# Attention's output product in seven block products per chunk, with weight sums made during attention

## The chip, the cores and the metric

The kernel runs on one core of one Trainium2 chip. The metric is the device time of one execution in microseconds (us). The engines are PE (matmul), PEld (its weight loads, which run beside PE), DVE (vector), ACT (scalar/activation), POOL (GpSimd) and SP, whose queue issues most DMAs. Times of the profile are counted from the start of the span, the stretch from the first to the last instruction of one profiled execution.

## The reference, cut to what matters

The computation is one step of a two-layer model over 256 context tokens and 1024 latent tokens, 1024 wide: first a gated linear attention layer (GLA), then a softmax attention layer with 8 heads of 128 and 2 key/value heads. The change concerns the last product of the attention layer:

```python
out_p = (attend_blocks(qp, kp, vp) * jax.nn.silu(gp)) @ att_w_out[i]
...
out_s = (attend_blocks(qs, keys, vals) * jax.nn.silu(gs)) @ att_w_out[i]
...
xp = xp + gt_p * out_p
xs = xs + gt_s * out_s
```

`att_w_out` is 1024 x 1024, all arrays are float32, and the rows are 256 + 1024 = 1280 tokens.

## The kernel before

**Number format.** A float32 operand is scaled by a power of two (`pow2`, from the largest magnitude) and split into two float16 parts: `hi` is an ACT copy with the scale, `lo` the rest, made by one DVE instruction from the float32 tile and `hi`. A product is then three matmuls for each 128 rows of the sum: hi·hi, hi·lo, lo·hi (`mm3`, line 247).

**The order of work.** All engines run their own queues in order. The order within a queue is chosen when the kernel is built, by a planner that simulates a timeline and takes instructions by program order plus an offset; the table `LATER` holds those offsets, by name of a step (`later("a.s0")`) and sometimes with an index. Memory of a closed pool is taken over by the next pool, and a tile there waits for the readers of the one that it replaces.

**The GLA loop** (about 100 to 475 us of the span). Beside its own work, `filler(slot)` fetches one 1 MB block of an attention weight (`stage`, into one of two `wst` tiles) in each slot of `AHEAD`, 14 in all, and `split_ahead` makes its scale (`scale`: four DVE reduces, `pow2`) and its split in four pieces of 512 elements, through the one `split` tile, and stores it in DRAM in float16 (`w_kv`, `w_q`, `w_g`, `w_o`). The last four blocks are the columns of `att_w_out` (`o0`, `o1`).

**Attention** (`attention`, about 700 to 1143 us). Ten steps n = 0 to 9, each one chunk of 256 tokens and one half of the heads; the second half takes the chunks in the order `OUT` = 1, 0, 2, 3, 4. A step has four heads e; a head has two `scores` (S in one of two three-bank tiles, maximum on DVE, exponential on ACT), two `rest` (the probabilities scaled and split on POOL or ACT and on DVE, then a DMA transposition from `phl` to `PT`) and, two heads later, `values`, which multiplies by the gate and stores the head's result in `og2_d`. `later` is a list of weight loads, one issued per head on SP. The split weights `o0` and `o1` are read back from step 6 and from step 9, into places that the gate and query weights have left. In step 9 the first chunk's row is loaded (`out2_load`) and prepared (`out2_prep`: two reduces, scale, split in two pieces of 1024) into the memory of `ropet`; after the ten steps two half tiles of chunk 1 (`out_piece`) are put among the last `values`.

**The last product** (`att_out`, about 1143 us to the end). Five chunks in the order `OUT`; a chunk has two token tiles, and a tile two halves of 512 output columns (`out_tile`, `residual`): 24 matmuls of 512 columns each into a bank `y`, then on DVE two multiplies (scale and gate) and one add of the residual row, and a store from ACT's queue. The next chunk's row is loaded and prepared beside the current chunk's matmuls.

Of the kernel before, what the change touches and what calls it, by code (L numbers as in the profile page):

```python
# [7 lines left out]
F16 = mybir.dt.float16  # L8
# [9 lines left out]
P = 128  # L18
# [26 lines left out]

OUT = (1, 0, 2, 3, 4)
# [18 lines left out]
    "a9.qr": 30,  # L65
    "a.s1": 30,
    "gate": -5,
    "a0.key": -85,
    "x.qr": -40,
    "z.val": 35,  # L70
    "o": -155,
    "x.q": -15,
    "a0.qr": 15,
# [3 lines left out]
    "a.q": -210,  # L77
    "x.mod": -60,
    "x.res": -225,
    "a.val": 20,  # L80
    "a9.gate": 5,
    "a9.q": -200,
    "a.s0": -25,
    "a.qr": -200,
    "a9.s1": -160,
    "a0.s1": 390,
    "pieces8": 95,
    "filler": -30,
    "a0.s0": 75,
    "at": -115,  # L90
    "a0.rest": 30,
    "a0.gate": 65,
    "silu": -150,
    "a9.s0": -20,
    "x.setup": -150,
    "a9.val": 5,
# [8 lines left out]
    "a0.q": 30,  # L105
    "wo3": 245,
    "x.key": -150,
# [14 lines left out]
    "a9.val.3": -80,  # L122
    "a.s0.1": -15,
    "a9.val.1": -5,
    "a9.rest.0": 25,
    "a9.rest.2": -60,
    "a.rest.0": 100,
    "a.val.1": 25,
    "z.val.0": -100,
    "a.q.0": -110,  # L130
    "a9.qr.1": 60,
    "z.val.1": 165,
    "a9.gate.2": 85,
    "a9.s1.0": -200,
    "a9.q.0": -210,
    "a9.gate.0": -5,
    "a9.q.2": 30,
    "a9.s1.2": -135,
    "a.s0.3": -100,
    "a.s1.0": 55,  # L140
    "a9.gate.3": 15,
    "a9.s1.3": -150,
    "z.prep": -5,
    "a9.s0.0": -25,
# [13 lines left out]
NAMES = ("kv", "q0", "g0", "q1", "g1", "o0", "o1")  # L158


class K:
# [36 lines left out]
    def pow2(self, mx, n=1, cross=True):  # L198
# [19 lines left out]
        nc.vector.tensor_scalar(s, e, -1, C268, ALU.mult, ALU.add)  # L218
        inv = self.t(sp, [P, n], I32, "p2i", bufs=12)
        nc.vector.tensor_scalar(inv, e, E14, None, ALU.subtract)  # L220
# [45 lines left out]
    def scale(self, st):  # L266
        nc = self.nc
        mx = self.t(self.small, [P, 4], F32, "wmx")
        for j in range(4):
            nc.vector.tensor_reduce(  # L270
                mx[:, j : j + 1], st[:, 2 * j : 2 * j + 2, :], AX.XY, ALU.max, apply_absolute_value=True
            )
        m = self.t(self.small, [P, 1], F32, "wm1")
        nc.vector.tensor_reduce(m, mx, AX.X, ALU.max)
        return self.pow2(m)
# [58 lines left out]


# [1024 lines left out]
    def rest(self, after=None):  # L1360
# [12 lines left out]
        if self.final:  # L1373
            parts = self.hT_lo[:, 0:2, :].rearrange("p k n -> p (k n)")
# [75 lines left out]
    def attention(self, wo, wk):  # L1450
# [4 lines left out]
        for n, (p, c) in enumerate(self.steps):  # L1455
# [4 lines left out]
            if n == 6:  # L1460
                wo.append(self.wload("o0", (0, 2), later))
            if n == 9:
                wo.append(self.wload("o1", 1, later))
            for e in range(4):
# [35 lines left out]
                if n == 9 and e == 1:  # L1500
                    xs, gs = ([self.hT_hi[:, a + j, 0:1024].bitcast(F32) for j in range(2)] for a in (0, 2))
                    with self.tc.issue_after(self.pt):
                        for j in range(2):
                            b = slice(512 * j, 512 * j + 512)
                            self.nc.sync.dma_start(gs[j], self.gt_d[1, 1:2, b].to_broadcast([P, 512]))
                            self.nc.sync.dma_start(xs[j], self.x1_d[2 * OUT[0], :, b])
                if n == 9 and e == 1:
                    first = self.ropet.rearrange("p a b d -> p (a b d)").bitcast(F16)
                    first = first.rearrange("p (j h t) -> p j h t", j=2, h=AH)
                    with self.later("z.prep"), self.tc.issue_after(self.last):  # L1510
                        self.prep = self.out2_prep(row, (first[:, 0], first[:, 1]))
        with self.tc.issue_after(self.pt):
            self.row, first = self.out2_load(OUT[1])
        with self.tc.issue_after(first):
            self.gt = self.gate_load(1)
        self.iw = self.inv_a[:, 10:14]
        wo[:] = [(hi, lo, 512) for hi, lo, _ in wo]
        for j, x in enumerate(xs):
            with self.later("z.out", f".{j}"):
                self.out_piece(OUT[0], 0, j, x, gs[j], wo)  # L1520
# [4 lines left out]
    def out2_load(self, c):  # L1525
        og = self.t(self.wst, [P, AH, 256], F32, "wst")
        return og, self.nc.sync.dma_start(og, self.og2_d[c]).ins

    def out2_prep(self, og, parts):
        nc = self.nc  # L1530
        hi, lo = parts
# [7 lines left out]
        s, inv = self.pow2(m)  # L1539
        for k in range(0, AH, 4):  # L1540
            nc.scalar.activation(hi[:, k : k + 4], og[:, k : k + 4], AF.Copy, scale=s)
            nc.vector.scalar_tensor_tensor(
                lo[:, k : k + 4], og[:, k : k + 4], s, hi[:, k : k + 4], ALU.mult, ALU.subtract
            )
        return hi, lo, inv

    def out_piece(self, c, j, cut, x, g, wo):
        nc = self.nc
        hi, lo, inv = self.prep
        i, a, b = 2 * c + j, slice(j * P, j * P + P), 512 * cut  # L1550
        o = self.O[0][0, i * P : i * P + P, :] if i < NTP else self.O[1][0, (i - NTP) * P : (i - NTP) * P + P, :]
        sc = self.t(self.small, [P, 4], F32, "rsc", bufs=2)
        nc.vector.tensor_scalar(sc, self.iw, inv, None, ALU.mult)
        ps = self.bank("mm")
# [400 lines left out]
```

## Time and profile before

| | |
|---|---|
| three runs | 1245.0, 1245.66, 1247.55 us; median 1245.66 |
| span of the profiled execution | 1240.9 us (the page gives no total of that execution beside it; the median run is 4.8 us longer than the span) |
| granted TensorE clock, mean | 0.997 |
| GLA loop | about 100 to 475 us |
| attention | about 700 to 1143 us |
| last product | 1143.7 us to the last DVE instruction at 1237.7 us |

A row of the table of stages gives the window, its length, then busy us and number of instructions of PE, PEld, DVE, ACT and POOL, the granted clock, the share of DMA time and GB/s. A group of instructions gives line, engine, operation, names written and read, shapes, count, then busy us, mean ns of one, idle us before and what ended it. In a tile's or a line's view the three numbers with slashes are the shortest, median and longest duration in ns. A DMA row ends in the median us from issue to landing. PE's busy time is modelled and covers short gaps.

### The profile page before, as it was taken

Reading aid. Unit: us, or ns where it says so; the run is one execution under the profiler, and the core shown is the slowest. Engines: PE = TensorE matmul, PEld = TensorE weight load, DVE = VectorE, ACT = ScalarE, POOL = GpSimd, SP = SyncE. Lnnn points to the kernel's source line nnn. Section 1 sums busy time; section 2 is a strip of 40 time slices with the busy share of each in tenths; the row PEclk is TensorE's granted clock in tenths of the full one; section 3 lists DMA queues with packets and bytes.
Section 4 is the critical chain, followed back from the end, with each engine's and each line's share of the span. In section 5 each row is a group of like instructions: output and inputs, shape, how many; then the busy total and the mean of one; then the engine's idle time right before and its main releaser. Section 6 shows DMA issues by size and latency. Waiting matters only on the chain. (4 is left out here: it accounts for less than half of the span.)

```text
span 1240.9 us, 22365 instructions
## 1 busy us (share of the span) xinstructions
PE 1190.7 (96%) x7990; PEld 778.3 (63%) x7990; DVE 944.9 (76%) x2177; ACT 687.0 (55%) x1694; POOL 320.5 (26%) x566
## 2 busy tenths in 40 slices
PE   5799999999999999799999999999999999989998
PEld 3467765655556566667776666776767666666444
DVE  4787779887888789976875787877767587786653
ACT  2565556665666657742333576666767676664110
POOL 0132122323321143311212443431322343311000
PEclk9999999999999999999999999999999999999999
DMA  9511566456555544489978787777958666979432
GB/s 378 196 69 73 196 202 228 127 185 203 175 191 164 189 132 161 112 186 307 204 174 203 178 163 138 132 145 133 199 124 161 124 118 132 205 139 246 158 137 85
DMA packets 318496, 210.14 MB, mean 169 GB/s; under 512 B 257158, under 2 KB 294702, under 8 KB 310064
## 3 DMA queue, kind: packets, MB, share of 16 engines
q1 hardware_dynamic: 311232, 191.18, 60.1%
q10 hardware_dynamic: 4688, 10.57, 2.2%
q0 software_dynamic: 2464, 6.95, 2.0%
q8 instruction: 63, 1.03, 0.3%
q14 instruction: 49, 0.40, 0.1%
HBM read 108.35 MB, written 38.96 MB: 119 GB/s over the span
## 5 line engine op out<-in xcount | busy, mean ns | idle before, releaser
L247 PEld LDWEIGHTS <-hT_hi 128*128 128x128 f16 x1920 | 187.6, 98 | 122.0 <-issue 5.6
L247 PE MATMUL mm<-whi,hT_hi 128*128 128x512 f16 (+1 forms) x576 | 200.2, 348 | 3.5 <-ACT gx L718 3.0
L247 PE MATMUL mm<-whi,hT_lo 128*128 128x512 f16 (+1 forms) x576 | 200.4, 348 | 0.0
L247 PE MATMUL mm<-wlo,hT_hi 128*128 128x512 f16 (+1 forms) x560 | 194.3, 347 | 0.7 <-DVE wlo L309 0.7
L247 PEld LDWEIGHTS <-whi 128*128 128x128 f16 x1232 | 120.3, 98 | 62.1 <-issue 2.2
L1344 PE MATMUL S<-kT,wst 128*128 128x512 f16 (+1 forms) x624 | 142.1, 341 | 4.1 <-ACT p L1352 4.0
L247 PE MATMUL mm<-hT_hi,whi 128*128 128x256 f16 (+1 forms) x480 | 141.1, 294 | 2.0 <-ACT gx L1392 2.0
L247 PE MATMUL mm<-hT_hi,wlo 128*128 128x256 f16 (+1 forms) x480 | 141.1, 294 | 0.0
L247 PE MATMUL mm<-hT_lo,whi 128*128 128x256 f16 (+1 forms) x480 | 141.1, 294 | 0.0
L1382 DVE SCALAR_TENSOR_TENSOR phl<-p,srec,phl 128x1280 f16<-128x1280 f32 (+1 forms) x79 | 105.3, 1332 | 40.6 <-ACT phl L1381 26.9
L247 PEld LDWEIGHTS <-hT_lo 128*128 128x128 f16 x960 | 94.1, 98 | 61.8 <-issue 1.1
L247 PE MATMUL mm<-PT,vh 128*128 128x256 f16 x672 | 114.6, 273 | 8.1 <-DMA PT<-phl 7.8
L1347 DVE TENSOR_REDUCE smx<-S 128x1 f32<-128x1280 f32 (+1 forms) x80 | 101.3, 1271 | 27.0 <-PE S L1344 26.9
L1352 ACT ACTIVATE p<-S,snb,acol 128x1280 f32<-128x1280 f32 (+1 forms) x80 | 99.1, 1239 | 12.5 <-DVE phl L1382 7.0
L1344 PEld LDWEIGHTS <-wst 128*128 128x128 f16 x624 | 61.4, 98 | 55.7 <-issue 6.9
L247 PE MATMUL mm<-PT,vl 128*128 128x256 f16 x336 | 91.6, 273 | 0.0
L1379 POOL TENSOR_SCALAR phl<-p,srec 128x1280 f16<-128x1280 f32 (+1 forms) x40 | 53.1, 1327 | 105.0 <-DVE srec L1370 57.1
L247 PEld LDWEIGHTS <-wlo 128*128 128x128 f16 x616 | 60.2, 98 | 29.2
L247 PEld LDWEIGHTS <-vh 128*128 128x128 f16 x672 | 65.1, 98 | 18.3 <-DMA PT<-phl 7.2
L1172 POOL TENSOR_TENSOR rope<-hx,ropet 128x64 f32<-128x64 f32 x160 | 51.2, 350 | 81.3 <-ACT hx L1308 63.8
L270 DVE TENSOR_REDUCE wmx<-wst 128x1 f32<-128x512 f32 x104 | 65.1, 677 | 3.5 <-DMA wst<-in_att_w 2.0
L238 POOL TENSOR_TENSOR hrs<-hrsa,mhalf 128x2 f32<-128x2 f32 x50 | 38.7, 775 | 106.8 <-DVE hrsa L236 106.5
(383 smaller groups left out, 2684.9 us busy)
## 6 DMA issues: line engine op xcount, KB each, us to landing
wada<-in_w_ada SPq DMA_DIRECT2D x16, 1024.0 KB, 5.4
wst<-in_att_w SPq DMA_DIRECT2D x14, 1024.0 KB, 5.3
wst<-in_gla_w_in SPq DMA_DIRECT2D x12, 1024.0 KB, 5.5
og_d<-og POOLq DMA_DIRECT2D x40, 128.0 KB, 2.8
wst<-og_d SPq DMA_DIRECT2D x5, 1024.0 KB, 6.0
og_d<-gx SPq DMA_DIRECT2D x37, 128.0 KB, 2.1
xr<-x_d SPq DMA_DIRECT2D x9, 512.0 KB, 3.3
out<-xr ACTq DMA_DIRECT2D x17, 256.0 KB, 2.0
```

Of the source, the lines that this page charges most:

```text
L238: nc.gpsimd.tensor_tensor(r, a, self.mhalf[:, 0:w], ALU.pow)
L247: self.pe = self.nc.tensor.matmul(out, a, b, start=k == 0 and j == 0, stop=k == n - 1 and j == 2).ins
L270: nc.vector.tensor_reduce(mx[:, j : j + 1], st[:, 2 * j : 2 * j + 2, :], AX.XY, ALU.max, apply_absolute_value=True)
L1172: nc.gpsimd.tensor_tensor(tv[:, h, :, w, :], xv[:, h, :, 1 - w, :], sn[:, :, w, :], ALU.mult)
L1344: nc.tensor.matmul(S[:, a : a + n], x, y, start=m == 0, stop=m == 2)
L1347: last = nc.vector.tensor_reduce(mx, S, AX.X, ALU.max).ins
L1352: nc.scalar.activation(p, S, AF.Exp, scale=self.sexp, bias=nb, accum_out=den)
L1379: nc.gpsimd.tensor_scalar(hi, p, r, 2.0 ** 14, ALU.mult, ALU.mult)
L1382: nc.vector.scalar_tensor_tensor(lo, p, r2, hi, ALU.mult, ALU.subtract)
```

## The change

The 256 tokens of a chunk, the 1024 rows of the sum and the 1024 columns are each taken in two halves, so that the chunk's product is one of 2 x 2 blocks. It is computed with seven block products and sums of blocks (the scheme of Strassen in Winograd's form), not eight block products.

*The weight.* `split_ahead` no longer handles `o0` and `o1`. Four blocks of `att_w_out`, each with 128 columns of either half, are fetched during attention, in steps 1, 3, 5 and 7 (`SPLIT`). At head 1 `split_out` makes the scale (with two bits of room for the sums) and splits three quarters as they are (B11, B21, B22); at head 3 `split_sums` makes four sums on POOL in place and splits them (T2, T3, T1, T4). Each part goes through one tile `opart` to `wo_d` in DRAM, 256 KB a store. Of the seven weights, 1 MB each, B11 and T2 are read back in step 8, T3, B21 and T1 in step 9, T4 and B22 in `att_out`.

*The rows.* `out2_prep` splits three of the chunk's four blocks as they are, makes four sums on POOL and splits those: seven ACT copies and seven DVE instructions of 512 elements. The first chunk is prepared in step 8.

*The products.* `product` has 12 matmuls of 512 columns; its moving operand is four pieces of 128 columns. `out_chunk` uses three banks: X, Y and Z. Products p6·T2 and p1·B11 are joined by an ACT copy and a DVE add, and later products add into a bank that DVE has changed. `finish` multiplies by the row's scale and the gate, adds the residual and stores, four times a chunk. The weight's scale goes into the gate row (`fold_gate`, POOL). Four products of the first chunk stand where the two half tiles did. The last head's split uses `ropet`.

Many offsets in `LATER` have other values and new names (`so`, `ss`, `e.t`, `e.prep`).

```diff
+SPLIT = (1, 3, 5, 7)
+PREPARE = 1
...
-NAMES = ("kv", "q0", "g0", "q1", "g1", "o0", "o1")
+NAMES = ("kv", "q0", "g0", "q1", "g1")
+B11, B21, B22, T2, T3, T1, T4 = range(7)
...
+    def split_part(self, g, s, m, b):
+        t = self.t(self.ew, [P, 2, 4, P], F16, "opart", bufs=1)
+        nc.scalar.activation(t[:, 0], b, AF.Copy, scale=s)
+        nc.vector.scalar_tensor_tensor(t[:, 1], b, s, t[:, 0], ALU.mult, ALU.subtract)
+        nc.sync.dma_start(self.wo_d[m, :, g], t.rearrange("p j k n -> p (j k n)"))
+
+    def split_out(self, g, st):
+        s, inv = self.scale(st, 2)
+        self.nc.vector.tensor_copy(self.inv_a[:, 10 + g : 11 + g], inv)
+        b11, b12, b21, b22 = self.quarters(st)
+        for m, b in ((B11, b11), (B21, b21), (B22, b22)):
+            self.split_part(g, s, m, b)
+        return s
+
+    def split_sums(self, g, st, s):
+        b11, b12, b21, b22 = self.quarters(st)
+        sub = self.nc.gpsimd.tensor_tensor
+        sub(b11, b12, b11, ALU.subtract)
+        sub(b12, b22, b12, ALU.subtract)
+        sub(b22, b22, b11, ALU.subtract)
+        sub(b21, b21, b22, ALU.subtract)
+        for m, b in ((T2, b22), (T3, b12), (T1, b11), (T4, b21)):
+            self.split_part(g, s, m, b)
...
     def attention(self, wo, wk):
...
-            if n == 6:
-                wo.append(self.wload("o0", (0, 2), later))
+            if n == 8:
+                self.out_weight(wo, later, ((m, t[:, :, 0:512]) for m, t in ((B11, self.hT_hi), (T2, self.hT_lo))))
             if n == 9:
-                wo.append(self.wload("o1", 1, later))
+                self.out_weight(wo, later, zip((T3, B21), self.wtile(1)))
+                self.out_weight(wo, later, ((T1, self.hT_hi[:, :, 512:1024]),))
...
+                if n in SPLIT and e == 0:
+                    st = self.stage(self.I["att_w"][10 + SPLIT.index(n)])
+                if n in SPLIT and e in (1, 3):
+                    with self.later(("so", "ss")[e // 2]):
+                        if e == 1:
+                            s = self.split_out(SPLIT.index(n), st)
+                        else:
+                            self.split_sums(SPLIT.index(n), st, s)
+                if n == 8 and e == 0:
+                    row = self.out2_load(OUT[0])
+                if n == 8 and e == PREPARE:
+                    parts = self.out_parts((0, 2))
+                    with self.later("z.prep"), self.tc.issue_after(self.last):
+                        ops = self.out2_prep(row, parts)
                 if n == 9 and e == 0:
-                    row = self.out2_load(OUT[0])[0]
...
+                    self.row = self.out2_load(OUT[1])
...
+        split(p1, a11)
+        split(p4, a22)
+        split(p2, a12)
+        sub(a22, a21, a22, ALU.add)
+        sub(a21, a11, a21, ALU.subtract)
+        sub(a11, a22, a11, ALU.subtract)
+        split(p6, a11)
+        split(p7, a21)
+        sub(a12, a12, a11, ALU.subtract)
+        split(p5, a22)
+        split(p3, a12)
...
+    def product(self, ps, a, w, start, halves=False):
+        for g0, g1 in ((0, 2), (2, 4)) if halves else ((0, 4),):
+            for k in range(4):
+                for j, (x, y) in enumerate(((0, 0), (0, 1), (1, 0))):
+                    self.pe = self.nc.tensor.matmul(
+                        ps[:, P * g0 : P * g1].rearrange("p (g n) -> p g n", n=P), a[:, x, k, :], w[:, g0:g1, y, k, :],
+                        start=start and k == 0 and j == 0, stop=k == 3 and j == 2, skip_group_check=True,
+                    ).ins
...
+    def out_chunk(self, c, ops, x, ts, ps, wo, last=False):
...
+        self.product(X, p1, wo[B11], True)
+        with self.later("e.t"):
+            nc.scalar.copy(t1, X2)
+        yield
+        self.product(Y, p6, wo[T2], True)
+        with self.later("e.t"):
+            nc.vector.tensor_tensor(Y2, Y2, t1, ALU.add)
+            nc.scalar.copy(t6, Y2)
+        yield
+        self.product(Z, p7, wo[T3], True)
+        with self.later("e.t"):
+            nc.scalar.copy(t7, Z2)
+        yield
+        self.product(X, p2, wo[B21], False)
+        yield
+        finish(X2, 0, 0)
+        self.product(Y, p5, wo[T1], False)
+        with self.later("e.t"):
+            nc.scalar.copy(t5, Y2)
+        nc.gpsimd.tensor_tensor(t5, t5, t7, ALU.add)
+        finish(t5, 1, 1)
+        yield
+        self.product(Z, p4, wo[T4], False)
+        nc.vector.tensor_tensor(Z2, Z2, t6, ALU.add)
+        finish(Z2, 1, 0)
+        yield
+        self.product(Y, p3, wo[B22], False, last)
...
     def att_out(self, wo):
+        tail = [(m, self.t(self.xp, [P, KT, 512], F16, f"wt{m}", bufs=1)) for m in (T4, B22)]
+        self.out_weight(wo, None, tail)
+        self.x += self.x_load(OUT[0])
         for n, c in enumerate(OUT):
-            if n + 1 < 5:
...
+            if n < 4:
+                row = self.row if n == 0 else self.out2_load(OUT[n + 1], (None, 0)[n % 2])
+                with self.later("e.prep", f".{n}"):
+                    nxt = self.out2_prep(row, self.out_parts(((2, 0), (0, 2))[n % 2]))
+                ts = [self.t(self.xp, [P, 2, 256], F32, f"ts{j}") for j in range(3)]
+                after = self.out_chunk(OUT[n + 1], nxt, self.x_load(OUT[n + 1]), ts, self.out_banks(), wo, n == 3)
+            for _ in self.chunk:
+                pass
+            self.chunk = after
```

More of the change, by code (lines that the diff above doesn't have):

```diff
@@ L196, in placed, with pow2 @@
             return f(*a)
[L198 removed]
+    def pow2(self, mx, n=1, cross=True, room=0):
         nc, sp = self.nc, self.small
@@ L263, in stage, with scale @@
         return st
-    def scale(self, st):
+    def scale(self, st, room=0):
         nc = self.nc
@@ L274, in scale @@
         nc.vector.tensor_reduce(m, mx, AX.X, ALU.max)
-        return self.pow2(m)
+        return self.pow2(m, room=room)
     def fill_out(self, w, st):
@@ L1538, in out2_prep @@
         nc.vector.tensor_tensor(m, mx[:, 0:1], mx[:, 1:2], ALU.max)
[L1539 to L1547, printed above, removed]
-        nc = self.nc
[L1549 to L1554, printed above, removed]
-        self.pieces(ps, lambda k: (hi[:, k, a], lo[:, k, a]), wo, b, 512)
-        for f in (0, 256):
-            t = ps[:, f : f + 256]
-            nc.vector.scalar_tensor_tensor(
-                t, t, sc[:, (b + f) // 256 : (b + f) // 256 + 1], g[:, f : f + 256], ALU.mult, ALU.mult
-            )
-        self.added = nc.vector.tensor_tensor(x, ps, x, ALU.add).ins
-        nc.scalar.dma_start(o[:, b : b + 512], x)
@@ L1564, in out_tile @@
[L1564 to L1573 removed]
+        s, inv = self.pow2(m, room=2)
```

256 lines of the change are left out of this document (163 added, 93 removed).

## Prediction

> **What bounds the kernel now.** I read the page first (span, busy times), then the table of busy time by stage, the waits of PE, the groups of the last tile `y`, and the chain that ended last. The page:
>
> ```profile
> span 1240.9 us, 22365 instructions
> PE 1190.7 (96%) x7990; PEld 778.3 (63%) x7990; DVE 944.9 (76%) x2177; ACT 687.0 (55%) x1694; POOL 320.5 (26%) x566
> ```
>
> Nothing but PE is near full. The median of the three runs, 1245.66 us, is 4.8 us above this span; the page gives no separate total for the profiled execution, so I work in the span and add 4.8 at the end. The stages, with busy times of PE, PEld, DVE, ACT, POOL, then clock, DMA share, GB/s:
>
> ```profile
> 100.00:475.00 375.00, 374.70 (x2291) 227.49 (x2289) 310.04 (x834) 229.78 (x599) 104.80 (x188) 1.00 0.54 174
> ...
> 700.00:1125.00 425.00, 410.82 (x2962) 289.20 (x2961) 326.15 (x621) 290.81 (x719) 137.98 (x227) 1.00 0.75 149
> ...
> 1126.00:1143.50 17.50, 17.11 (x111) 10.51 (x109) 10.64 (x20) 4.17 (x9) 0.00 (x0) 1.00 1.05 255
> 1143.50:1240.90 97.40, 93.64 (x460) 44.65 (x460) 50.50 (x101) 8.75 (x8) 1.07 (x2) 1.00 0.38 133
> ```
>
> The GLA loop (100 to 475), attention (700 to 1125) and the last product (1143.5 on) all have PE at 96 to 100%. What PE waited for, first in the GLA loop, then in attention (total, times, longest):
>
> ```profile
> PE mm L247 <- ACT gx L718: 3.0, 1, 3.0
> PE z L865 <- POOL Sc L830: 1.1, 2, 0.9
> ...
> PE mm L247 <- DMA PT<-phl: 7.8, 6, 3.3
> PE S L1344 <- ACT p L1352: 4.0, 6, 2.3
> PE mm L247 <- ACT gx L1392: 2.0, 1, 2.0
> PE mm L205 <- DVE wm L1538: 0.4, 1, 0.4
> ```
>
> Attention loses 14.2 us of 425 to waits, the GLA loop under 8. The last product, from the chain that ended last:
>
> ```profile
> 1143.67 15.97 PE y L247 x74
> ...
> 1159.70 16.84 PE y L247 x78
> ...
> 1176.59 18.99 PE y L247 x88
> ...
> 1195.64 41.51 PE y L247 x216
> ...
> 1237.70 0.42 DVE xr L1030
> ```
>
> It is an unbroken run of matmuls from 1143.67 to 1237.16; nothing else stands on this path. 16.84 / 78 and 18.99 / 88 both give 0.216 us from one 512-column matmul to the next.
>
> **The removed matmuls.** A chunk is 256 tokens: before, 2 token tiles x 2 column halves x 8 rows of blocks x 3 (hi·hi, hi·lo, lo·hi) = 96 matmuls of 512 columns, 20.7 us. After, a block product has 4 rows of blocks x 3 = 12, and there are seven: 84, or 18.1 us. Over five chunks 60 matmuls go: 60 x 0.216 = **-13.0 us**, on the path that ends the kernel. Of each chunk 0, two half tiles before and four block products after (48 matmuls either way) lie ahead of the final run, so the run shrinks by all 60. The cross-partition matmuls of the scales are as many as before (four for weights, five for rows), the last chunk's DVE ending (a 256-column multiply and add) too.
>
> One thing could take from this: the moving operand was 512 neighbouring columns and is now four pieces of 128, 2 KB apart. No row has that form; I take the same pitch, and the other end stands among the rivals. The Trainium skill (SBUF — State Buffer, Door 1: The DMA port swizzle) says that reads slow down when successive elements leave a 16-byte line; pieces of 128 neighbouring half-width numbers fill such lines, so by it the pitch stays; no run here shows it yet.
>
> **The GLA loop.** Four weight stages leave it (loads, scales, splits, and 16 stores past SP's queue). Each stage has 4 reduces, about 1.3 us of small scale steps, and 4 splits:
>
> ```profile
> L270 DVE TENSOR_REDUCE wmx<-wst x104: 670/676/686, 14.9 to 463.4; 128x1 f32<-128x512 f32 x104
> L329 ACT ACTIVATE split<-wst,p2s x56: 705/713/739, 127.0 to 452.1; 128x512 f16<-128x512 f32 x56
> L330 DVE SCALAR_TENSOR_TENSOR split<-wst,p2s,split x56: 736/748/1044, 128.1 to 453.9; 128x512 f16<-128x512 f32 x56
> L333 SPq DMA_DIRECT2D w_o<-split x16: 359/370/377, 374.5 to 454.8; - x16
> ```
>
> The small steps are the reduce over partitions and seven of 0.15 (rows below). That is 4 x (2.7 + 1.3 + 3.0) = 28 us of DVE and 11.4 of ACT, but off the path: PE is busy 374.70 of 375.00. It can give at most the waits there (7.3 with the five smaller ones), and a new order of the loop can cost one wait like the longest (3.0). I take **-1.0**, between -7.3 and +3.0, nearest to the 0.3 that the stage's busy time leaves.
>
> **Attention gets the stages back, dearer.** Each now makes seven parts of 512 elements, not four, and four sums on POOL. DVE: 4 x (2.7 + 1.3 + 7 x 0.748) = 37 us; ACT: 28 x 0.713 = 20. For a POOL sum of 512 the near rows are
>
> ```profile
> L793 POOL TENSOR_TENSOR at<-am x40: 452/484/872, 92.0 to 497.5; 128x128 f32<-128x128 f32 x40
> L1172 POOL TENSOR_TENSOR rope<-hx,ropet x160: 307/319/1562, 592.1 to 1070.2; 128x64 f32<-128x64 f32 x160
> ```
>
> From 64 to 128 elements the shortest grows from 307 to 452 ns, 2.27 ns each, so 512 take 452 + 384 x 2.27 = 1.32 us; stretched as the longest L793 is against its shortest (872 / 452), 2.5. Take 1.32, as the median is near the shortest: 16 x 1.32 = 21 us. On the stage's 425 us DVE goes from 326 to 363 (85%), ACT from 291 to 311 (73%), POOL from 138 to 159 (37%): none is full. DMA gets 4 MB of loads, 7 MB of stores (before 4 MB, in the GLA loop) and 7 MB to read back, for 4; at 0.75 busy there is room on average.
>
> So the cost isn't work but waits. All 28 parts go through one staging tile (`opart`, one buffer): a part's ACT copy waits until the store of the part before has landed, and what ACT holds behind it is the exponential of the scores, which frees the bank that PE writes scores into. The same arrangement stood in the GLA loop with 28 fillings of `split`; there it gave
>
> ```profile
>   DMA w_o<-split: 5.2, 3
>   DMA w_q<-split: 3.3, 3
> ...
>   DMA w_kv<-split: 1.8, 1
>   DMA w_g<-split: 1.6, 1
> ```
>
> (us and times of ACT's and DVE's idle time ahead of `split`; of the first, the longest is the third number here:)
>
> ```profile
> ACT split L329 <- DMA w_o<-split: 5.2, 3, 3.2
> ```
>
> 11.9 us in all, 0.43 us a filling, and PE's waits there name no split. In attention PE does wait for the exponential (4.0 us above) and for the transposes (7.8), which share SP's queue with the 28 stores. Bounds: -3 (a new order may also remove a wait of the 14.2) and +12 (all 11.9 reaches PE). I take a quarter, **+3.0**, since most of what ACT loses falls beside other PE work.
>
> The row of the first chunk is now prepared in step 8 instead of 9: one 1 MB load, two reduces and the splits move past SP and DVE work that has the same slack, and leave step 9. Cost nothing; without the cover it is the 8.7 us of DVE worked out below. The last head's split goes to `ropet`, whose last reader is done by then: nothing.
>
> **The last product's own work.** Per chunk DVE had eight 256-wide multiplies and four adds, and per preparation two reduces and two splits of 1024:
>
> ```profile
> L1027 DVE SCALAR_TENSOR_TENSOR y<-y,rsc,wst 128x256 f32<-128x256 f32 x36 | 17.7, 491 | 28.6 <-PE y L247 28.2
> L1030 DVE TENSOR_TENSOR xr<-y,xr 128x512 f32<-128x512 f32 (+1 forms) x19 | 12.6, 664 | 0.5
> L1542 DVE SCALAR_TENSOR_TENSOR wlo<-wst,p2s,whi 128x1024 f16<-128x1024 f32 x8 | 9.9, 1282 | 4.9 <-ACT whi L1541 4.9
> L1534 DVE TENSOR_REDUCE wmx<-wst 128x1 f32<-128x1024 f32 x6 | 7.0, 1214 | 9.7 <-DMA wst<-og_d 9.7
> ...
> L210 DVE TENSOR_REDUCE p2m<-mm 128x1 f32<-128x128 f32 x4 | 1.1, 287 | 0.0
> L218 DVE TENSOR_SCALAR p2s<-p2e 128x1 int32<-128x1 int32 x4 | 0.6, 152 | 0.1
> ```
>
> After: four 512-wide multiplies (I estimate 0.76: 0.491 for 256 columns plus the 0.27 by which the add grows from 0.42 to 0.69), four adds and two more adds between products (0.69 each), 7.2 us. The preparation has two reduces (2.4), about 1.1 of scale steps and seven splits of 0.748: 8.7. Together 15.9 of a chunk's 18.1 us, where it was some 13 of 20.7. ACT: four copies and seven splits, under 8; POOL: five sums, 6.6. PE stays the bound, but with 2.2 us of DVE slack a chunk. Waits inside a chunk: T1 adds into the bank of T2 after one DVE add and one ACT copy (some 1.5 us), with two products (5.2 us) between; B22 needs the ACT copy of T1's result, with one product (2.6 us) between. Both fit, unless a queue is late.
>
> Two weights (T4, B22) are loaded only when attention's buffers are free, which is after the last value matmul. From issue to landing the two kinds of load took (last column)
>
> ```profile
> wst<-gt_d SPq DMA_DIRECT2D x4, 512.0 KB, 7.1
> ...
> whi<-w_q SPq DMA_DIRECT2D x1, 1024.0 KB, 6.8
> ```
>
> the row nearest to the folding of the gate row is
>
> ```profile
> L565 POOL TENSOR_SCALAR hT_hi<-h x8: 617/732/951, 39.9 to 67.7; 128x512 f16<-128x512 f32 x8
> ```
>
> and the gate row's issue and the last value matmul stand in order of time at
>
> ```profile
> 1134.97 0.92 SPq L1012 DMA_DIRECT2D wst<-gt_d  x2
> ...
> 1142.77 0.27 PE L247 MATMUL mm<-PT,vl 128*128 128x256 f16 x1
> ```
>
> T4 is issued near 1142.8 and lands near 1149.6. The T1 product covers 2.6 us, and the next chunk's first five (13 us) cover the rest if the order puts them there: 0 to 4.2. The gate row lands late too (1135 + 7.1 = 1142) and is folded on POOL, four steps of about 0.73; behind that wait only DVE's endings of chunk 0, and PE has the other three banks. For this whole stage **+2.0**, between 0 and the 7.8 that the DVE rival below would take.
>
> **Sum:** -13.0 - 1.0 + 3.0 + 2.0 = -9.0; the span becomes 1231.9 and the time 1231.9 + 4.8 = **1236.7 us**, against the median 1245.66.
>
> **The rivals.**
> *Slower: the staging tile sets attention's pace.* Place: ACT's in-order queue, at each of 28 fillings. For: the stores of `w_o`, the very ones moved, held ACT 5.2 us in 8 fillings, 0.65 each, in a stage with a DMA share of 0.54, and attention has 0.75. Against: 28 fillings over 425 us leave 15 us for each. If 0.65 each reaches PE, 18.2 us come back: -13.0 - 1.0 + 18.2 + 2.0 = +6.2, 1251.9. It decides above (13.0 + 1.0 - 2.0) / 28 = 0.43 us a filling.
>
> *DVE and POOL in each other's way at the end.* The longest L330 split is 1044 ns against 736, and the longest ones all overlap POOL instructions. Seven splits longer by 0.3 make 18.0 us of DVE work in an 18.1 us chunk; with 1.2 us of waits for ACT (the 4.9 above, over four preparations) DVE sets the pace, at up to the old 20.7. On the three chunks with a preparation beside them 7.8 us return in place of the 2.0: 1242.5. Against: the median split is 748. The Trainium skill (GPSIMD Engine Reference, 8. Key points) says that POOL shares its way into SBUF with the Vector engine and collides with Vector instructions that read two SBUF inputs, which the splits are. By that rule this case is the outcome wherever POOL's sums and the splits meet; the trace agrees in kind (1044 against 736) but not in most rows.
>
> *Late data around the switch.* T4 uncovered (4.2) and one more transposition wait like the longest (3.3) behind the 3 MB of weights now read in step 9: 7.5 in place of 2.0, 1242.2.
>
> *The change doesn't do what it says:* four pieces of 128 columns cost four short matmuls. From the chain, with 256-column matmuls alone in it:
>
> ```profile
> 1098.63 6.07 PE mm L247 x54
> ```
>
> 0.1124 us each, 0.0044 over half of 0.216; three starts more in each of 420 matmuls are 5.5 us: 1242.2. Nothing speaks for it but the form.
>
> *Better:* attention and the end hide everything, the loop gives 3: -16.0, 1229.7.
>
> **How the numbers follow.** Chances: forecast 0.48, staging tile 0.16, DVE and POOL 0.13, late data 0.10, pieces 0.04, better 0.09. From no change a measurement can tell about 0.2%, 2.5 us: faster is under 1243.2. Of the staging case a quarter ends within that; of DVE-and-POOL and late data about 0.07 together. Faster 0.77, same 0.11, slower 0.12. The range leaves out half of "better" and 0.13 of the staging case: 1230.5 to 1246; the forecast's own range is 1232 to 1241.
>
> **What would show it.** In the profile after: 420 matmuls of 512 columns in the last product at a pitch of 0.216 (0.229 for the pieces); the final run near 80 us, without gaps over 1 us between block products; PE's waits in attention near 17 us, and no ACT wait of many us on the store of `opart`; POOL's 512-wide sums at 1.3 us; the splits of the last stage near 0.75. Wrong would make it: ACT waiting on `opart` at every part, the exponential late, PE waiting for scores; or PE waiting for DVE at each block product; or a stretch without matmuls where T4 is due.

## The result, and the profile after

The changed kernel takes 1288.85 us (median of 4 runs, 1283.79 to 1290.7) against 1245.74 us for the kernel before: a ratio of 1.034, 95% interval 1.0315 to 1.0364. It is 43 us slower where 9 us faster was forecast, and the time lies outside the range. The profiled execution took 1288.44 us, 2.2 us more than its span. Its page:

```profile
span 1286.2 us, 22399 instructions
...
PE 1195.8 (93%) x7918; PEld 778.5 (61%) x7918; DVE 979.8 (76%) x2194; ACT 724.7 (56%) x1751; POOL 392.0 (30%) x611
```

PE has 72 instructions fewer, and DVE's share is 76% as before. These shares tell nothing of 45 us more in the span (the medians differ by 43; a profile is of one execution). Three marks in PE's queue place them (us from the start of the span, worked out from the first and last instruction of each kind):

| | before | after | difference | forecast |
|---|---|---|---|---|
| start to the first score matmul (with the GLA loop) | 696.5 | 696.3 | -0.2 | -1.0 |
| first score to the last value matmul (attention) | 446.3 | 500.1 | +53.8 | +3.0 |
| last value matmul to the end (last product) | 98.2 | 89.8 | -8.4 | -11.0 |

The table of stages after, columns as before:

```profile
100.00:475.00 375.00, 375.00 (x2292) 227.71 (x2290) 295.53 (x803) 226.64 (x600) 106.20 (x190) 1.00 0.48 154
700.00:1125.00 425.00, 382.86 (x2629) 262.07 (x2627) 329.04 (x639) 286.57 (x697) 158.15 (x229) 0.96 0.73 157
...
1197.00:1286.00 89.00, 81.05 (x387) 37.15 (x385) 68.75 (x110) 28.44 (x45) 31.61 (x23) 1.00 0.47 169
```

In the GLA loop DVE's busy time falls from 310.04 to 295.53 us in the window, and PE stays full: nothing was to be had there. In attention PE falls from 410.82 to 382.86 and the granted clock from 1.00 to 0.96. DVE is busy 329.04 of 425 us, where the kernel before had 326.15, so its own table row shows no engine that is full. (The window is fixed and holds less of the longer stage. From the first score to the last value matmul DVE was busy 339.8 of 446.3 us before and 382.1 of 500.1 after: 42.3 us more, and 76% both times.) The waits of PE in attention (total, times, longest), 700 to 1180 us:

```profile
PE mm L288 <- DMA PT<-phl: 16.6, 10, 4.0
PE S L1414 <- ACT p L1422: 14.8, 7, 5.2
PE mm L288 <- DVE og L1477: 5.8, 5, 3.1
PE mm L288 <- DVE srec L1442: 4.4, 2, 2.7
```

PE waits for transposed probabilities (7.8 us before), for the exponential (4.0 before), and for DVE itself (0.4 before). The waits of DVE tell more than its share. Before, 700 to 1125 us, its largest:

```profile
DVE smx L1347 <- PE S L1344: 26.9, 28, 4.1
DVE phl L1382 <- ACT phl L1381: 26.9, 25, 2.7
DVE phl L1382 <- POOL phl L1379: 11.8, 9, 2.6
```

After, in the same window:

```profile
DVE phl L1452 <- POOL phl L1449: 20.1, 13, 3.5
DVE opart L385 <- ACT opart L384: 13.5, 10, 2.9
...
DVE smx L1417 <- PE S L1414: 12.0, 11, 2.2
```

Before, the maximum of the scores (`smx`) waited 28 times for PE: DVE was ahead of the bound engine there, by 26.9 us in all. After, it waits for PE 11 times and 12.0 us: mostly the scores lie ready and DVE comes late. Most of DVE's other idle time ends with its partners in the same head's chain (POOL's and ACT's half of the split); that this time was not free is what the experiments have to show.

### The profile page after: what moved, and what is told of

It is laid out like the page before. It is cut to its first block, busy times and chain, and to the rows that moved or that the text cites. A ratio compares the mean times of both kernels' runs of the same rounds, so it can differ in the third digit from the quotient of the medians.

```text
span 1286.2 us, 22399 instructions
## 1 busy us (share of the span) xinstructions
PE 1195.8 (93%) x7918; PEld 778.5 (61%) x7918; DVE 979.8 (76%) x2194; ACT 724.7 (56%) x1751; POOL 392.0 (30%) x611
## 3 DMA queue, kind: packets, MB, share of 16 engines
q8 instruction: 62, 1.02, 0.3%
## 5 line engine op out<-in xcount | busy, mean ns | idle before, releaser
L288 PE MATMUL mm<-PT,vh 128*128 128x256 f16 x672 | 128.6, 286 | 24.1 <-DMA PT<-phl 16.6
L1414 PE MATMUL S<-kT,wst 128*128 128x512 f16 (+1 forms) x624 | 135.0, 342 | 15.4 <-ACT p L1422 14.8
L1452 DVE SCALAR_TENSOR_TENSOR phl<-p,srec,phl 128x1280 f16<-128x1280 f32 (+1 forms) x79 | 115.1, 1459 | 38.8 <-POOL phl L1449 24.2
L288 PEld LDWEIGHTS <-whi 128*128 128x128 f16 x960 | 94.8, 99 | 43.2 <-issue 11.6
L288 PE MATMUL mm<-PT,vl 128*128 128x256 f16 x336 | 95.9, 285 | 0.0
L288 PEld LDWEIGHTS <-vh 128*128 128x128 f16 x672 | 67.9, 103 | 42.1 <-issue 22.5
L1242 POOL TENSOR_TENSOR rope<-hx,ropet 128x64 f32<-128x64 f32 x160 | 59.8, 402 | 77.5 <-ACT hx L1378 52.3
L431 ACT ACTIVATE ls<-ls 128x256 f32<-128x256 f32 (+1 forms) x81 | 33.1, 409 | 49.0 <-DVE ls L424 48.7
```

The source lines that it names most:

```text
L288: self.pe = self.nc.tensor.matmul(out, a, b, start=k == 0 and j == 0, stop=k == n - 1 and j == 2).ins
L431: nc.scalar.activation(u, u, AF.Exp)
L1242: nc.gpsimd.tensor_tensor(tv[:, h, :, w, :], xv[:, h, :, 1 - w, :], sn[:, :, w, :], ALU.mult)
L1414: nc.tensor.matmul(S[:, a : a + n], x, y, start=m == 0, stop=m == 2)
L1452: nc.vector.scalar_tensor_tensor(lo, p, r2, hi, ALU.mult, ALU.subtract)
```

## The experiments

All times are medians, and each ratio is against runs of the kernel before on the same chip. The start of each step's first maximum on DVE (`smx`) serves as a mark, and its "lag" is against the kernel before.

**Round 1: offsets, weight work or stores.** Theory A: the one staging tile and its stores hold ACT. Theory B: the re-planned order. Theory C: the added engine work.

The kernel before with the changed kernel's offsets:

```diff
 LATER = {
-    "a9.qr": 30,
-    "a.s1": 30,
+    "a9.qr": -480,
+    "a.s1": 50,
 ...
```

> The kernel before with nothing changed but the table of offsets, which takes the changed kernel's values (new names have no step here). Theory A, the one staging tile: after's attention is slow because ACT waits 32.0 us for the stores of opart, so the table alone costs little: 1243 to 1252 us. Theory B, the order: the changed offsets give attention a bad order whatever work is in it; then this kernel loses most of what the change lost (43 us), 1270 to 1290. Theory C, the added 37 us of DVE and 20 us of ACT work in attention: like A, 1243 to 1252.

1277.39 us, ratio 1.0257 [1.0234, 1.0281]. The first score comes 9 us later and attention takes 24 us longer, with no instruction added. The order alone is worth up to 32 us.

The changed kernel with the offsets of before (the new names kept):

> The changed kernel with the offsets of the kernel before wherever that has the name; the offsets of the new steps (so, ss, e.t, e.prep) stay. Theory A (staging tile): the tile is the same, 1275 to 1295 us. Theory B (order): the loss in attention goes, 1235 to 1248. Theory C (work): 1275 to 1290.

1302.01 us, 1.0457 [1.044, 1.0475]: 13 us worse than with its own offsets. The new offsets suit the new work; they do not explain its cost.

The changed kernel without the weight work in attention; the last product then reads other stored weights of the same size, so that its output is not the reference's:

```diff
-                if n in SPLIT and e == 0:
-                    st = self.stage(self.I["att_w"][10 + SPLIT.index(n)])
-                if n in SPLIT and e in (1, 3):
...
-            src = self.wo_d[m].rearrange("p g (j n) -> p (g j) n", j=2)
+            src = self.stand_in[:, m % 2]
```

> The changed kernel with its own offsets, but attention makes no part of the output weight: no stage loads, scales, sums, splits or stores (28 ACT, 28 DVE splits, 16 reduces, 16 POOL sums and 28 stores less). The seven weights are read from the stored query weights instead, so that part of the computation is left out. Theory A and theory C: attention is as in the kernel before and the whole gain of the last product shows, 1233 to 1240 us. Theory B (order): still 1260 to 1280.

1255.21 us, 1.0086 [1.0067, 1.0105]. The last value matmul comes at 1162.1, against 1196.4 with the work: the weight work costs 34 us at these offsets. The other 19 us against before's 1142.8 are there without it; 16 of them appear between DVE's first maximum of step 8 and that of step 9, where 9 us more of matmuls stand, too.

Everything but the 28 stores (the same stand-in weights):

```diff
         nc.vector.scalar_tensor_tensor(t[:, 1], b, s, t[:, 0], ALU.mult, ALU.subtract)
-        nc.sync.dma_start(self.wo_d[m, :, g], t.rearrange("p j k n -> p (j k n)"))
```

> The changed kernel with its own offsets and all the weight work in attention, without the 28 stores; the seven weights are read from the stored query weights instead, so the product is with other weights. A part's ACT copy then waits for DVE's reading of the part before and for no store. Theory A (staging tile): 32.0 us of ACT's waits go, 1238 to 1250 us. Theory B (order): 1270 to 1285. Theory C (work): the DVE and ACT instructions are all there, 1275 to 1290.

1291.08 us, 1.0371 [1.0353, 1.0388]: nothing gained. Its waits, of PE and then of ACT, 700 to 1180 us:

```profile
PE mm L288 <- DMA PT<-phl: 29.7, 9, 7.1
PE S L1413 <- ACT p L1421: 14.8, 10, 4.3
```

```profile
ACT snb L1418 <- DVE smx L1416: 58.4, 35, 6.1
...
ACT opart L384 <- DVE opart L385: 13.7, 10, 2.8
```

ACT now waits at `opart` for DVE's read of the part before, not for a store, and 58.4 us for the maximum. Theory A falls as the cause of the loss. In the changed kernel itself that wait is real, though, and can be followed once to PE. Its total (ACT, 700 to 1180 us) is

```profile
ACT opart L384 <- DMA wo_d<-opart: 32.0, 16, 3.9
```

and around 911 us three queues in order of time (start, duration, what; in brackets the idle time before it and what ended it), SP, ACT and PE:

```profile
904.12 7.08 SPq L1453 DMA_TRANSPOSE PT<-phl  x2
911.29 0.54 SPq L386 DMA_DIRECT2D wo_d<-opart  x1
```

```profile
915.31 0.72 ACT L384 ACTIVATE opart<-wst,p2s 128x512 f16<-128x512 f32 x1 [3.86 <-DMA wo_d<-opart]
```

```profile
918.13 0.80 PE L1414 MATMUL S<-kT,wst 128*128 128x256 f16 x3 [5.22 <-ACT p L1422]
```

The store stands behind two transpositions, the next part's copy behind the store, the exponential behind the copy, and PE behind the exponential: 5.22 us. This is the staging rival's mechanism, as it was described. Taken away, another wait takes its place.

**Round 2: which part of the work.** Without weight work and with the old offsets:

> As the kernel without weight work (1255.2 us), with the offsets of the kernel before wherever that has the name. Theory B2, order and work both cost: the new offsets alone cost the kernel before 32 us, so the old ones should give here 1233 to 1245 us. Theory C2, the work alone matters and offsets are noise: 1250 to 1260.

1249.81 us, 1.0034 [1.0016, 1.0052]. Up to the first maximum of step 9 the lag is -3 us; the last value matmul is 12 us late (1154.8). Of these 12, 5.2 are not a loss: 72 matmuls of the last product lie ahead of that mark here, where the changed kernel has 48. Against the run with the work at the same offsets, the weight work costs 52 us.

All weight work, the sums too, in the GLA loop, as `split_ahead` had it, with the old offsets:

```diff
+        cols += [(None, j, I["att_w"][10 + j]) for j in range(4)]
...
+                    k.jobs.append((k.split_ahead, name, j, st) if name else (k.split_ahead_sums, j, st))
```

> The whole computation with seven block products, but the four weight stages (scale, sums on POOL, seven splits, stores) stay in the GLA loop, where the kernel before has its output weight stages; offsets of the kernel before. Theory C2 or B2: attention loses its 37 us of DVE work again and the last product keeps its gain, 1235 to 1250 us. If the seven products themselves cost attention its time (late weights, early preparation): over 1255.

1295.01 us, 1.0404 [1.0375, 1.0434]. The first score comes 37 us late, and from there to the first maximum of step 9 the lag stays between 36 and 41 us: so far attention is as fast as before. Step 9 then loses 12 us more (5.2 of them the matmuls of the run above). So place matters only in where the loss falls. The loop, which this prediction saw as having PE full, is no better a home; on 100 to 475 us its row is

```profile
100.00:475.00 375.00, 367.23 (x2226) 220.76 (x2225) 310.55 (x803) 223.78 (x577) 117.75 (x192) 0.99 0.53 173
```

and ACT's wait for the staging tile there is 17.5 us in 8 (`split`). PE's idle time in this row is 7.8 us, so most of the 37 us falls behind 475 us. Why 9 us more DVE work and 21 us of POOL sums cost that much was not taken apart.

The weight work without copies, splits and stores (loads, scales and POOL sums stay):

```diff
     def split_part(self, g, s, m, b):
-        t = self.t(self.ew, [P, 2, 4, P], F16, "opart", bufs=1)
...
+        pass
```

> The changed kernel with its own offsets; the weight stages in attention keep their loads, scales (16 reduces, 16 us of DVE in all) and POOL sums, and leave out the 28 splits (20 us ACT, 21 us DVE) and stores; the weights are read from the stored query weights instead. Theory DVE load: the loss of 34 us between no weight work and all of it shrinks with DVE's share, 16 of 37: about 1270 us. Theory POOL sums (they hold up POOL's probabilities): 1280 to 1290. Theory ACT load (20 us gone): 1255 to 1260.

1273.5 us, 1.0226 [1.02, 1.0251]: 18 us above the run without any, for 16 of the 37 us of DVE work. Half the DVE work costs half the loss, with POOL's sums still there.

Without the four sums (the parts are split unsummed, so other numbers are multiplied):

```diff
-        sub(b11, b12, b11, ALU.subtract)
-        sub(b12, b22, b12, ALU.subtract)
-        sub(b22, b22, b11, ALU.subtract)
-        sub(b21, b21, b22, ALU.subtract)
```

> The changed kernel with its own offsets without the 16 sums on POOL (the parts are split as they are, so that the weights are wrong sums). Theory DVE load: 1283 to 1290, as with the sums. Theory POOL sums: 1255 to 1265.

1303.31 us, 1.0476 [1.0446, 1.0506], slower than with them by 14 us. So nothing speaks for POOL's sums as the cause. A kernel with less work that takes longer also shows the scatter of this method: each edit makes the planner order the instructions anew. That this is where the 14 us come from was not shown; other offsets alone made 13 us in the changed kernel and 32 in the kernel before.

**Round 3: the suspected work alone, in the kernel before.** Here nothing of the change is present. 28 instructions without use are added in steps 1, 3, 5 and 7, on the heads where the weight parts would be made:

```diff
+                if n in (1, 3, 5, 7) and e in (1, 3):
+                    for d in range(3 if e == 1 else 4):
+                        self.nc.vector.tensor_reduce(self.t(self.small, [P, 1], F32, "dummy"), self.ropet[:, 0], AX.XY, ALU.max)
```

> The kernel before with 28 DVE maxima of 1024 elements (about 1.21 us each, 34 us) added in attention at the places of the 28 parts (3 at head 1, 4 at head 3 of steps 1, 3, 5, 7); they read a constant table and nobody reads their result. No ACT, POOL or DMA work, old offsets. Theory DVE load: most of it reaches PE, +25 to +40: 1270 to 1286 us. Theory ACT load or DMA: under +5, 1245 to 1251. Theory order (any inserted instruction breaks the planned order): as much as with tiny instructions in the next run.

> The same 28 places with a copy of one element per partition (about 0.15 us each, 4 us in all): the order is planned anew, the load hardly grows. Theory DVE load: 1245 to 1251 us. Theory order: 1265 to 1285.

> The kernel before with 28 ACT copies of 512 elements (about 0.71 us each, 20 us) at the same places, into a tile nobody reads. Theory DVE load: under +5, up to 1251 us. Theory ACT load (ACT holds the exponentials): +12 to +25, 1258 to 1270.

> The kernel before with both: 28 ACT copies and 28 DVE maxima, 20 and 34 us, near the ACT and DVE work of the weight stages (20 and 37), without their waits on each other, their sums on POOL, their loads and stores. Theory load: at least what the weight work costs the changed kernel, +34 to +55: 1280 to 1300 us. If the coupling (ACT before DVE, one tile, stores) is what costs: under +20, below 1266.

28 DVE maxima of 1.21 us: 1275.21, 1.0234 [1.0219, 1.025]. 28 DVE instructions of 0.14 us: 1250.14, 1.0028 [1.0014, 1.0042]. 28 ACT copies of 0.63 us: 1250.56, 1.0042 [1.0026, 1.0059]. Maxima and copies together: 1291.49, 1.0356 [1.0328, 1.0383], or 46 us, 11 more than the two add up to. The rows of `dummy` showed a flaw, though: nothing held the instructions to their heads, and the maxima ran bunched from 698 to 738 us. So the runs were made again with each instruction issued behind its head's work.

```diff
+                        with self.tc.issue_after(self.last):
```

> In the earlier run the added maxima all ran between 698 and 738 us, ahead of their places. Here each is held behind the scores of its head (3 at head 1, 4 at head 3 of steps 1, 3, 5, 7), as the weight parts are: 28 x 1.21 = 34 us of DVE. Theory DVE load: +25 to +40, 1270 to 1286 us. Theory bunching (the earlier +30 came of 34 us within 40 us): under +12, below 1258.

> The same 34 us of DVE work as 36 maxima of 768 elements (about 0.94 us), one held behind the scores of each head of steps 0 to 8. Theory DVE load: as in the held lumps within 8 us, since the total is the same. Theory lumps (three or four in a row hold up a maximum that PE waits for): under half of what the lumps cost.

> 28 ACT copies of 512 elements (about 0.63 us here, 18 us in all) held at the same places as the lumps. Theory DVE load: under +5, up to 1251 us. Theory ACT load: +12 to +25, 1258 to 1270.

> 28 copies of one element on DVE (0.14 us each, 4 us) held at the same places: the order is planned anew and hardly any load is added. Theory DVE load: +3 to +5, up to 1251 us. Theory order: +15 or more.

Held, the 28 maxima ran from 767 to 1066 us: 1274.98 us, 1.0225 [1.0199, 1.025]. 28 tiny ones at the same places: 1250.0, 1.0028 [1.0012, 1.0044]. 36 maxima of 0.94 us, one on each head: 1266.63, 1.0162 [1.0136, 1.0187]. The ACT copies (1251.41, 1.0042 [1.0025, 1.0058]) ran bunched again, from 698 to 751 us, so how ACT work spread over attention would do was not measured. The row of attention with the held maxima, the group of the maxima, and the waits of PE and of DVE:

```profile
700.00:1125.00 425.00, 392.24 (x2759) 270.90 (x2757) 329.57 (x612) 276.42 (x696) 136.79 (x224) 0.99 0.68 139
```

```profile
L1501 DVE TENSOR_REDUCE dummy<-ropet 128x1 f32<-128x1024 f32 x28 | 32.1, 1207 | 0.0
```

```profile
PE S L1344 <- ACT p L1352: 11.4, 10, 2.6
PE mm L247 <- DMA PT<-phl: 10.1, 6, 3.6
PE mm L247 <- DVE og L1407: 6.0, 5, 1.4
```

```profile
DVE phl L1382 <- ACT phl L1381: 29.4, 26, 2.7
DVE smx L1347 <- PE S L1344: 19.7, 13, 4.6
DVE phl L1382 <- POOL phl L1379: 18.7, 12, 2.4
```

This is the picture of the changed kernel, in kind, made by DVE work alone: 34 us are added, DVE's busy time in the window rises by 3.4 us (326.15 to 329.57), and PE's falls by 18.6. DVE is not full at 78%: it gets through fewer heads in the same window. Over the whole of attention it is busy 365.4 of 475.2 us, 77%, where it was 76%. Waits for `p`, `PT` and `og` come up, and the lag grows in the steps that hold the work: 1.6 us at step 1, 2.2, 4.0, 11.0, 7.3, 21.3, 17.5, 28.4, 29.0 at step 9. Against the tiny instructions 28 x 1.066 = 29.8 us more DVE time cost 25.0 us. Spread evenly, 33.9 us cost 21.3, so lumps take about 8 of the 30.

**Round 4: the best order for both.** Old offsets for steps 0 to 8 and the new ones for step 9 and the end; first without weight work (stand-in weights as above), then the whole change:

> No weight work in attention (weights read from the stored query weights, that part is left out), with the old offsets for steps 0 to 8 and the new ones for step 9, the hand-over and the last product (names a9, z and e). With old offsets alone attention kept its time up to step 9 and then lost 12 us at the hand-over; with the new ones the end took 8.4 us less than before. If both hold side by side: 1232 to 1242 us. If the hand-over costs time whatever its offsets (late T4 and B22, the banks held by the last scores): 1246 to 1256.

> The whole changed kernel with the same mixed offsets. Theory DVE load: the weight work costs about what it cost there, 29 to 54 us over the kernel above: 1270 to 1295 us.

Without weight work 1243.6 us, 0.9991 [0.9974, 1.0008]; whole, 1292.04 us, 1.0372 [1.0334, 1.0411]. The weight work costs 48 us between them. Even if the weights were free, this order would only reach the kernel before. Its row of the end and its first waits of PE, 1100 to 1250 us:

```profile
1152.00:1241.00 89.00, 80.72 (x386) 36.98 (x383) 68.52 (x109) 28.43 (x45) 31.61 (x23) 1.00 0.46 169
```

```profile
PE mm L273 <- DMA PT<-phl: 1.8, 3, 1.3
PE mm L231 <- DVE wm L1603: 1.8, 1, 1.8
PE y L1645 <- ACT whi L1608: 1.1, 1, 1.1
```

It ends 89.8 us after its last value matmul, as the changed kernel does. It runs 3 us ahead up to the first maximum of step 8; at that of step 9 it is 7.8 us behind, and the last value matmul comes at 1151.1, 8.3 late. Steps 8 and 9 as rows (columns as before), first the kernel before, then this run:

```profile
1043.30:1086.70 43.40, 42.98 (x325) 31.43 (x323) 35.15 (x63) 31.02 (x78) 16.78 (x28) 1.00 0.83 179
1086.70:1142.80 56.10, 51.68 (x383) 36.96 (x380) 43.87 (x70) 30.96 (x54) 7.65 (x8) 1.00 0.89 189
```

```profile
1040.70:1094.50 53.80, 47.54 (x356) 34.43 (x354) 47.61 (x80) 36.98 (x87) 24.05 (x32) 0.99 0.80 174
1094.50:1151.10 56.60, 50.41 (x347) 34.61 (x347) 33.48 (x51) 28.41 (x52) 13.10 (x12) 0.92 0.81 172
```

The two steps have the same matmuls in both kernels (708 and 703 records in the rows) and take 110.4 us where they took 99.5. Step 8, which now holds the first chunk's preparation (its seven splits run from 1074 to 1092), has 12.5 us more DVE work and takes 10.4 us longer; step 9 has 10.4 us less of it and is no shorter, at a clock of 0.92. No version that was run beats the kernel before by more than its measurement can tell.

## Why the prediction was wrong

**The step that failed** is "Attention gets the stages back, dearer", at "none is full. So the cost isn't work but waits." It was forecast as +3.0 us, with +12 as its bound and 18.2 as the staging rival's price, and was +53.8. The share of 85% for DVE was taken as room. It was not: in attention PE's scores, DVE's maximum, ACT's exponential, the split on three engines, the transposition and PE's values follow each other, and DVE's remaining time was for the most part waiting inside that chain. Work of DVE alone, put into the kernel before, cost 30 us for 34 (25 against tiny instructions at the same places, 21 spread evenly). The weight work, with 37 us of DVE and 20 of ACT, cost 34, 48 and 52 us in three pairs of equal offsets. What of it is ACT's part, or DVE's own waits for ACT's half of a part (`opart`, 13.5 us above), was not separated. What the prediction could have read is the row of `smx` above: of 99 us that DVE was idle, 26.9 us were ended by PE's scores, less than the 37 us to be added. That this number is the limit was argued, not shown: the held maxima used up only 7 us of it and still cost 30.

**A second step failed** in the same part: "The row of the first chunk is now prepared in step 8 instead of 9 ... Cost nothing". Only the last three of the 28 weight parts run in steps 8 and 9, yet these take 114.4 us in the changed kernel, 15.0 more than before; steps 0 to 7 take the other 38.8. Without any weight work they take 11 us more than before with the mixed offsets, and with the old ones 10 (114.3, less 5.2 for the matmuls taken over from the last product); there step 8 keeps its time (42.8 us, DVE busy 40.4 of it) and step 9 loses it. The preparation, which the prediction priced at 8.7 us of DVE without cover, lies in step 8 in both. That it is the cause is argued from its place and size; no run moved it alone.

**Where the 53.8 us are.** From one matmul of attention to the next, the time beyond the usual pitch (0.216 us for 512 columns, 0.109 for 256, twice that at half clock), summed over the trace, rose from 17.1 to 58.0 us (+40.9), and the half clock itself cost 14.8 us where it was 1.6 (+13.2). That makes 54.1. By cause: 34 us come with the weight work (the changed kernel against the run without it), and 19 are there without it, from the order and from steps 8 and 9. With the old offsets that rest was 7 (12 less 5.2), with the mixed ones 8.

**DVE and POOL in attention.** The prediction saw these two collide only at the end. In the changed kernel eight of DVE's 63 splits of 1280 probabilities took 2.42 to 2.59 us, where the longest before was 1.61; five of the eight lay beside sums that the change gave POOL, the other three beside POOL's own split. It is 8 us of DVE work that no term held. It is not what decides: with the old and the mixed offsets only two and one took over 2.4 us, and these kernels were no faster.

**The staging tile** was the rival that ended on the right side, and its place and chain are in the trace. Its price (0.65 us a filling) was too small against 32.0 us of ACT waits, and as a cause it fell: without the stores the time is 2 us longer (1291.08 against 1288.85).

**The removed matmuls** were right. The chain that ended last, 1190 to 1290 us:

```profile
1191.09 5.18 PE y L1666 x24
...
1203.27 1.72 POOL wst L1637
...
1207.12 1.43 DVE whi L1630
...
1245.49 9.73 PE y L1666 x45
```

5.18 / 24 and 9.73 / 45 are 0.216 us, with a moving operand of four pieces: the rival of the pieces falls, and -13.0 stands. This agrees with the rule of the Trainium skill that was weighed (SBUF — State Buffer, Door 1: The DMA port swizzle).

**The last product's own work** was forecast at +2.0 between 0 and 7.8. From one matmul to the next, the time beyond the pitch is 4.0 us there, nearly all of it in five gaps from 1206 to 1245 us, against 0.5 before (+3.5), and the ending after the last matmul's start takes 5.1 us, not 4.1. So -13.0 + 3.5 + 1.1 = -8.4, as measured, and the term was +4.6. The waits in the gaps:

```profile
PE mm L246 <- DVE wm L1624: 1.8, 1, 1.8
PE y L1666 <- ACT whi L1629: 1.0, 1, 1.0
PE y L1666 <- ACT ts L1694: 0.5, 1, 0.5
```

That points to the rival of DVE and POOL, at some six tenths of its 7.8; no run took the collisions away. The splits of the rows after:

```profile
L1630 DVE SCALAR_TENSOR_TENSOR whi<-wst,p2s,whi x12: 735/746/1690, 1122.2 to 1245.1; 128x512 f16<-128x512 f32 x12
...
L1630 DVE SCALAR_TENSOR_TENSOR wlo<-row,p2s,wlo x6: 733/744/1678, 1221.5 to 1266.8; 128x512 f16<-128x512 f32 x6
```

Of all 35, the 17 that lay beside POOL instructions for 30% of their time or more took 1086 ns on average, the other 18 took 741. Against this rival the prediction leaned on a median of 748 ns; the medians are the same here, and hide the half that collides.

**The GLA loop** gave 0.2 of 1.0 us, as the 0.3 us of idle time in its row allowed.

Of POOL's four sums for each block in attention two took 1.26 to 1.27 us, near the 1.32 estimated, and the two others 1.59 and 1.83 on average; one of either kind:

```profile
L400 POOL TENSOR_TENSOR wst<-wst 128x512 f32<-128x512 f32 x4 | 7.3, 1827 | 0.2
...
L399 POOL TENSOR_TENSOR wst<-wst 128x512 f32<-128x512 f32 x4 | 5.1, 1267 | 0.0
```

## What to carry to other kernels

Room on an engine that stands in a chain with the bound engine is not its idle share: look at what ends its idle time, and count as free at most what the bound engine ends (here not even that was had: 34 us of work used up 7 of the 26.9 and cost 30). Before work is moved into such a stage, put dummy instructions of that length there and time them; it is one edit, and here it gave 21 to 30 us where +3.0 was forecast for the stage. In a kernel whose order is planned, an edit is judged only beside a control with the same kind of edit: 28 tiny instructions moved the time by 5 us, other offsets by 13 to 32.

## What the hardware showed unexpectedly

A wait of PE cost more than its length. Around the wait of 5.22 us shown above the stages read (PE's columns and the granted clock):

```profile
914.50:918.00 3.50, 0.00 (x0) 0.00 (x0) 1.09 (x2) 2.69 (x10) 1.22 (x4) 0.81 0.77 186
918.00:921.40 3.40, 3.27 (x16) 2.33 (x16) 3.25 (x11) 3.22 (x13) 2.88 (x7) 0.50 0.29 79
```

In the 3.4 us after the wait the clock is 0.50, and matmuls run at half pace: 0.21 us from one of 256 columns to the next, and 0.11 from 925 us on. In attention such stretches, six of 3.41 and two of 6.83 us, came 8 times (34.1 us) in the changed kernel and once (3.4 us) before, and cost the 13 us named above: one third on top of the added idle time. The Trainium skill (TensorE: Matmul & The Clock Gate, Part 1: The HAM clock gate) states windows of 3413 ns, after an idle one of which the clock is halved until a busy one has passed; the length of these stretches agrees. An idle window need not be an empty one, though: five of the eight followed waits of only 2.1 to 3.1 us, and up to 1.3 us of the 3.41 before a stretch were filled with matmuls.
